# Channel-major projections: both parts of the activations streamed as 512 columns under one high weight tile

## The chip, the cores and the metric

The kernel runs on one core of one Trainium2 chip. The metric is the device time of one execution in microseconds (us); lower is better. Runs of the kernel before took 1342.85, 1344.12 and 1344.26 us, so the median is 1344.12 us.

## What is computed

Two layers of a decoder trunk, for 256 tokens of 1024 channels, all in float32. Cut to what matters here:

```python
def swiglu(x, w_gu, w_down):                     # w_gu: 1024 x 5632, w_down: 2816 x 1024
    gate, up = jnp.split(x @ w_gu, 2, axis=-1)
    return (jax.nn.silu(gate) * up) @ w_down

def hybrid_layer(x, mem_n, ...):
    h = layer_norm(ALPHA * x + 0.5 * swiglu(x, ffn1_w_gu, ffn1_w_down), ...)
    (dn_q, dn_k, dn_v, dn_b, dn_a, dn_z, sw_q, sw_k, sw_v, xa_q, gates) = jnp.split(h @ w_in, split_idx, axis=-1)
    o_dn = deltanet_branch(...)                  # causal convolution + silu of q, k, v, then a chunked recurrence
    o_sw = sliding_window_attention(...)
    o_xa = memory_cross_attention(xa_q, mem_n, w_mem_kv)
    merged = jnp.sum(gates * jnp.einsum('bsnc,ncd->bsnd', branches, w_branch), axis=2)
    h = layer_norm(ALPHA * h + merged @ w_out, ...)
    return layer_norm(ALPHA * h + 0.5 * swiglu(h, ffn2_w_gu, ffn2_w_down), ...)
```

Each layer has two feed-forwards (`swiglu`) with the three mixers between them, so the whole has four feed-forwards and two mixer stages.

## The kernel before

**Split operands.** TensorE works on the type float32r here. To keep float32 accuracy every operand is split into a high part (a cast to float32r) and a low part (the value less its high part), and a product is three matmuls: high x high, high x low, low x high. `split` (L115) does this with one cast on ScalarE (ACT, L116) and one subtraction on VectorE (DVE, L117).

**Weights.** All weights come from HBM as one stream of units of 128 x 1024 numbers (512 KB) through `unit` (L99): a DMA on SyncE's queue into a ring of three raw buffers, then a `split` into a ring of five high (`whi`) and five low (`wlo`) tiles. A cast into a `whi` buffer waits until TensorE (PE) has done the matmuls of the unit five places earlier. Every unit costs one ACT cast and one DVE subtraction of 128 x 1024.

**Two kinds of projection.** `projA` (L140) is token-major: the activations are the stationary operand, 512 weight columns stream. It does the down-projections, gates, branch projections and the output projection. `projB` (L125) is channel-major: a 128 x 128 weight tile is the stationary operand and the 256 tokens of the transposed activations stream. For each of 8 row tiles k and each 128-channel tile t it issues three matmuls of 256 columns: L135 (high weights, high activations), L136 (high weights, low activations), L137 (low weights, high activations). All three add into the same 256 columns of a PSUM bank; a bank holds two channel tiles.

**Where projB is used.** In a feed-forward (`Ffn.rest`, L312) the columns f = 2..21 are done by one `projB` each, with two channel tiles (gate and up) and two weight units: 16 (k, t) pairs. Then `glu` (L305) takes the silu of the gate on ACT (L307) and multiplies by the up half on DVE (L309), both read from PSUM, and a `split` of 128 x 256 makes the operand of the down-projection. In a mixer stage `projB` makes the memory keys, the delta-net's k, q and v (followed by `conv`, L416: one scaled copy on ACT and three multiply-adds on DVE for each 128-channel tile, L421 and L424, read from PSUM), the two queries and the window's keys: five calls of four channel tiles and one of one tile on the stream, one of four on the memory.

**PSUM.** Eight banks: `acc` has four tiles of one bank, `at` and `sm` two each. `full_rows` (L177) takes four `acc` and one `at` for a down-projection of 256 x 1024: `a` and `b` for the first 128 tokens, `c`, part of `d` and `at` for the second.

**What sets the order.** The tile framework schedules the instructions onto in-order queues, one for each engine; weight splits have a raised priority, so they run ahead of other work. An instruction at the head of a queue that waits holds everything behind it on that engine.

Of the kernel before, what the change touches and what calls it, by code (L numbers as in the profile page):

```python
# [17 lines left out]
P = 128  # L18
# [20 lines left out]
def tile_trunk(ctx, tc, x, xT, mem, wst, lnp, memln, cvw, rows, cst, out):  # L39
# [8 lines left out]
    psA = ctx.enter_context(tc.tile_pool(name="psA", bufs=4, space=bass.MemoryType.PSUM))  # L48
# [13 lines left out]
    def acc():  # L62
        return T(psA, [P, 512], "acc")
# [61 lines left out]
    def projB(xt, nt, kpu, behind=None):  # L125
        banks = [acc().rearrange("p (t s) -> p t s", t=2) for _ in range((nt + 1) // 2)]
        for uu in range(KD // kpu):
            hi, lo = unit(behind=behind)
            for kk in range(kpu):
                k = uu * kpu + kk  # L130
                for t in range(nt):
                    c = (kk * nt + t) * P
                    o = banks[t // 2][:, t % 2, :]
                    lastt = t % 2 == 1 or t == nt - 1
                    nc.tensor.matmul(o, hi[:, c:c + P], xt[0](k), start=(k == 0 and t % 2 == 0), stop=False, skip_group_check=True)  # L135
                    nc.tensor.matmul(o, hi[:, c:c + P], xt[1](k), start=False, stop=False, skip_group_check=True)  # L136
                    nc.tensor.matmul(o, lo[:, c:c + P], xt[0](k), start=False, stop=(k == KD - 1 and lastt), skip_group_check=True)  # L137
# [51 lines left out]
    def new_hT():  # L189
        hi = T(pu, [P, KD, S], "hThi", F32R)  # L190
        lo = T(pu, [P, KD, S], "hTlo", F32R)
        return hi, lo

    def acc_of(t):
        return (lambda k: t[0][:, k, :], lambda k: t[1][:, k, :])

    def to_T(put, tb, src, q):
        # half q of src (P, 1024), token-major, to its place in the transposed pair
# [4 lines left out]
        hi, lo = put(q)  # L203
# [720 lines left out]
```

## Time and profile before

| | |
|---|---|
| median of 3 runs | 1344.12 us (1342.85 to 1344.26) |
| the profiled execution, first to last instruction | 1340.6 us |
| mean granted TensorE clock | 0.994 |
| PE / PEld busy | 97% / 89% of the span |
| DVE / ACT / POOL busy | 63% / 49% / 4% |
| read from HBM | 235.64 MB, 178 GB/s over the span |

The profiled execution's span is 3.5 us below the median of the runs; what lies before the first and after the last instruction is not in it.

A profile line names the program line, the engine, the operation, what it writes and reads, the shapes and the count; then the total busy time and the mean of one in ns, then idle time before them and what ended it. PE is TensorE's matmul, PEld its weight loads. The busy time of a matmul includes its way through the array, which overlaps with the next one, so the pace of matmuls is read from the distance of their starts in the timeline, not from the busy time.

### The profile page before, as it was taken

Reading aid. Unit: us, or ns where it says so; the run is one execution under the profiler, and the core shown is the slowest. Engines: PE = TensorE matmul, PEld = TensorE weight load, DVE = VectorE, ACT = ScalarE, POOL = GpSimd, SP = SyncE. Lnnn points to the kernel's source line nnn. Section 1 sums busy time; section 2 is a strip of 40 time slices with the busy share of each in tenths; the row PEclk is TensorE's granted clock in tenths of the full one; section 3 lists DMA queues with packets and bytes.
Section 4 is the critical chain, followed back from the end, with each engine's and each line's share of the span. In section 5 each row is a group of like instructions: output and inputs, shape, how many; then the busy total and the mean of one; then the engine's idle time right before and its main releaser. Section 6 shows DMA issues by size and latency. Waiting matters only on the chain.

```text
span 1340.6 us, 22696 instructions
## 1 busy us (share of the span) xinstructions
PE 1304.8 (97%) x9112; PEld 1190.9 (89%) x9112; DVE 851.1 (63%) x1346; ACT 662.3 (49%) x1015; POOL 49.1 (4%) x75
## 2 busy tenths in 40 slices
PE   8999999999899999999999999999979999999997
PEld 7999889997678789998899998899977787999986
DVE  5585466777675775554665554757875758655545
ACT  6544344566464444444454443445656645444441
POOL 0000000102001000000000000000020010000000
PEclk9999999999899999999999999999999999999999
DMA  8867565653235736555665555566532457465553
GB/s 262 267 201 250 188 204 168 211 179 89 81 126 170 230 127 206 180 188 188 220 219 190 188 179 190 182 186 208 158 105 74 140 188 236 126 191 187 183 188 116
DMA packets 68585, 240.39 MB, mean 179 GB/s; under 512 B 8160, under 2 KB 9312, under 8 KB 68480
## 3 DMA queue, kind: packets, MB, share of 16 engines
q1 hardware_dynamic: 66176, 232.53, 54.0%
q0 software_dynamic: 2304, 6.43, 1.6%
q8 instruction: 71, 1.16, 0.4%
q14 instruction: 34, 0.28, 0.1%
HBM read 235.64 MB, written 3.28 MB: 178 GB/s over the span
## 4 chain that ended last, share of the span: by engine, by line
PE 77%; DMA 9%; DVE 8%; ACT 3%; issue 2%; POOL 1%; SPq 0%; DVEq 0%; ACTq 0%; POOLq 0%
PE acc L136 15%; PE acc L135 15%; PE acc L137 15%; PE acc L122 8%; PE acc L121 8%; PE acc L123 8%; DMA raw<-in_wst_dram 7%; DVE wlo L117 3%; ACT whi L116 2%; DMA w<-dr 1%; PE sm L644 1%; PE at L123 1%; PE at L121 1%; PE at L122 1%; PE sm L202 1%
## 5 line engine op out<-in xcount | busy, mean ns | idle before, releaser
L117 DVE TENSOR_TENSOR wlo<-raw,whi 128x1024 fp32r<-128x1024 f32 (+2 forms) x403 | 484.9, 1207 | 359.5 <-ACT whi L116 356.5
L116 ACT CAST whi<-raw 128x1024 fp32r<-128x1024 f32 (+2 forms) x403 | 414.9, 1033 | 413.0 <-DMA raw<-in_wst_dram 111.9
L135 PE MATMUL acc<-hThi,whi 128*128 128x256 f32 x1616 | 458.1, 284 | 0.0
L136 PE MATMUL acc<-hTlo,whi 128*128 128x256 f32 x1616 | 457.5, 283 | 0.0
L137 PE MATMUL acc<-hThi,wlo 128*128 128x256 f32 x1616 | 457.3, 283 | 0.0
L136 PEld LDWEIGHTS acc<-hTlo,whi 128*128 128x128 f32 x1616 | 310.3, 192 | 0.0
L135 PEld LDWEIGHTS acc<-hThi,whi 128*128 128x128 f32 x1616 | 310.3, 192 | 0.0
L137 PEld LDWEIGHTS acc<-hThi,wlo 128*128 128x128 f32 x1616 | 310.1, 192 | 0.0
L122 PE MATMUL acc<-wlo,u 128*128 128x512 f32 (+1 forms) x400 | 149.8, 375 | 0.0
L121 PE MATMUL acc<-whi,u 128*128 128x512 f32 (+1 forms) x400 | 149.0, 372 | 0.0
L123 PE MATMUL acc<-whi,u 128*128 128x512 f32 (+1 forms) x400 | 147.8, 371 | 0.0
L121 PE MATMUL acc<-whi,hThi 128*128 128x512 f32 (+1 forms) x272 | 103.5, 381 | 5.2 <-ACT whi L116 5.2
L122 PE MATMUL acc<-wlo,hThi 128*128 128x512 f32 (+1 forms) x272 | 103.2, 379 | 0.0
L123 PE MATMUL acc<-whi,hTlo 128*128 128x512 f32 (+1 forms) x272 | 103.1, 379 | 0.0
L121 PEld LDWEIGHTS acc<-whi,u 128*128 128x128 f32 x400 | 75.4, 188 | 13.8 <-DVE t L309 0.8
L122 PEld LDWEIGHTS acc<-wlo,u 128*128 128x128 f32 x400 | 75.4, 189 | 12.5
L123 PEld LDWEIGHTS acc<-whi,u 128*128 128x128 f32 x400 | 74.9, 188 | 12.7
L116 ACT CAST u<-t 128x256 fp32r<-128x256 f32 x80 | 32.5, 406 | 99.5 <-DVE t L309 99.3
L121 PEld LDWEIGHTS acc<-whi,hThi 128*128 128x128 f32 x272 | 52.2, 192 | 14.9 <-ACT whi L116 5.2
L123 PEld LDWEIGHTS acc<-whi,hTlo 128*128 128x128 f32 x272 | 51.9, 191 | 9.6 <-issue 1.6
L122 PEld LDWEIGHTS acc<-wlo,hThi 128*128 128x128 f32 x272 | 52.0, 191 | 8.6 <-DVE wlo L117 0.9
L117 DVE TENSOR_TENSOR u<-t,u 128x256 fp32r<-128x256 f32 x80 | 34.0, 425 | 32.6 <-ACT u L116 32.6
(312 smaller groups left out, 1489.0 us busy)
## 6 DMA issues: line engine op xcount, KB each, us to landing
raw<-in_wst_dram SPq DMA_DIRECT2D x409, 512.0 KB, 3.6
raw<-in_wst_dram SPq DMA_DIRECT2D x16, 324.0 KB, 3.1
gB<-in_lnp_dram SPq DMA_DIRECT2D x6, 512.0 KB, 6.3
bB<-in_lnp_dram SPq DMA_DIRECT2D x6, 512.0 KB, 5.7
mdr<-w POOLq DMA_DIRECT2D x4, 512.0 KB, 8.6
w<-dr POOLq DMA_DIRECT2D x4, 512.0 KB, 9.0
w<-mdr POOLq DMA_DIRECT2D x4, 512.0 KB, 5.6
t<-in_xT_dram SPq DMA_DIRECT2D x4, 256.0 KB, 5.2
```

Source lines behind the costliest of these rows:

```text
L116: nc.scalar.copy(hi, src)
L117: nc.vector.tensor_tensor(lo, src, hi.bitcast(F32), op=ALU.subtract)
L121: nc.tensor.matmul(o, lh, rh, start=first, stop=False, skip_group_check=skip)
L122: nc.tensor.matmul(o, lh, rl, start=False, stop=False, skip_group_check=skip)
L123: nc.tensor.matmul(o, ll, rh, start=False, stop=last, skip_group_check=skip)
L135: nc.tensor.matmul(o, hi[:, c:c + P], xt[0](k), start=(k == 0 and t % 2 == 0), stop=False, skip_group_check=True)
L136: nc.tensor.matmul(o, hi[:, c:c + P], xt[1](k), start=False, stop=False, skip_group_check=True)
L137: nc.tensor.matmul(o, lo[:, c:c + P], xt[0](k), start=False, stop=(k == KD - 1 and lastt), skip_group_check=True)
L202: nc.tensor.transpose(ps[:, j * P:(j + 1) * P], src[:, k * P:(k + 1) * P], ident)
L644: together(lambda h: nc.tensor.matmul(ps[:, h, :], *f(h), start=True, stop=True))
```

## The change

Five things change together.

1. `new_hT` makes one tile in which the high and the low activations of a row tile k lie side by side: 512 columns. The memory's transposed tiles are laid out the same way.
2. `projB` issues two matmuls instead of three for each (k, t): one of 512 columns under the high weight tile (its result: high x high in the first 256 columns, high x low in the last 256 of a full PSUM bank), and one of 256 columns under the low weight tile into the first half. It takes at most two channel tiles a call, so calls of four become two calls of two with half the units each; the weights are laid out in memory to suit (`_stream`).
3. A new `total` adds the halves when they are read: an ACT copy of the second half to SBUF and a DVE addition of the first. What follows (`glu`, `conv`, `split`) then reads SBUF.
4. `acc` has two tiles of two banks instead of four of one; `full_rows`, the feed-forward's first columns and the gates share such tiles.
5. `glu` writes in place of its operands in `Ffn.rest`.

```diff
-    psA = ctx.enter_context(tc.tile_pool(name="psA", bufs=4, space=bass.MemoryType.PSUM))
+    psA = ctx.enter_context(tc.tile_pool(name="psA", bufs=2, space=bass.MemoryType.PSUM))
...
     def acc():
-        return T(psA, [P, 512], "acc")
+        return T(psA, [P, 2, 512], "acc")
...
     def projB(xt, nt, kpu, behind=None):
-        banks = [acc().rearrange("p (t s) -> p t s", t=2) for _ in range((nt + 1) // 2)]
+        b = acc().rearrange("p t (a s) -> p t a s", a=2)
         for uu in range(KD // kpu):
             hi, lo = unit(behind=behind)
             for kk in range(kpu):
                 k = uu * kpu + kk
                 for t in range(nt):
                     c = (kk * nt + t) * P
-                    o = banks[t // 2][:, t % 2, :]
-                    lastt = t % 2 == 1 or t == nt - 1
-                    nc.tensor.matmul(o, hi[:, c:c + P], xt[0](k), start=(k == 0 and t % 2 == 0), stop=False, skip_group_check=True)
-                    nc.tensor.matmul(o, hi[:, c:c + P], xt[1](k), start=False, stop=False, skip_group_check=True)
-                    nc.tensor.matmul(o, lo[:, c:c + P], xt[0](k), start=False, stop=(k == KD - 1 and lastt), skip_group_check=True)
-        return banks
+                    nc.tensor.matmul(b[:, t], hi[:, c:c + P], xt[2](k), start=k == 0, stop=False, skip_group_check=True)
+                    nc.tensor.matmul(b[:, t, 0], lo[:, c:c + P], xt[0](k), start=False, stop=k == KD - 1, skip_group_check=True)
+        return b[:, 0:nt]
+
+    def total(b):
+        y = T(p2, [P, b.shape[1], S], "t2", bufs=4)
+        nc.scalar.copy(y, b[:, :, 1])
+        nc.vector.tensor_tensor(y, y, b[:, :, 0], op=ALU.add)
+        return y
+
+    def projB_split(xt, parts, behind=None):
+        for i in range(2):
+            split(*(t[:, 2 * i:2 * i + 2, :] for t in parts), total(projB(xt, 2, 4, behind)))
...
     def full_rows():
-        a, b, c, d = (acc() for _ in range(4))
-        return [[a, b], [c, d[:, 0:S], at()[:, 0:S]]]
+        a, b = acc(), acc()
+        return [[a[:, 0], a[:, 1]], [b[:, 0], b[:, 1, 0:S], at()[:, 0:S]]]
...
     def new_hT():
-        hi = T(pu, [P, KD, S], "hThi", F32R)
-        lo = T(pu, [P, KD, S], "hTlo", F32R)
-        return hi, lo
+        t = T(pu, [P, KD, 2, S], "hT", F32R)
+        return t[:, :, 0, :], t[:, :, 1, :], t
...
             for f in range(2, NFT):
-                (b,) = projB(xt, 2, 4, behind if f == 2 else None)
-                hf = self.glu(b[:, 0, :], b[:, 1, :])
+                gu = total(projB(xt, 2, 4, behind if f == 2 else None))
+                hf = self.glu(gu[:, 0], gu[:, 1], gu[:, 0], gu[:, 1])
...
         def conv(seg, dst):
-            for i, b in enumerate(projB(xt, 4, 2)):
+            for i in range(2):
+                b = total(projB(xt, 2, 4))
```

**The ACT queue in the feed-forward.** One column f, near the end of the first layer's second feed-forward; `acc` is what `projB` wrote, `t` the SBUF tile, `u` the down-projection's operand, `whi` a high weight tile. Before:

```order
L116 CAST whi_6424<-raw_6423 128x1024 [waits DMAHW7_49,PE_49,Activation_49]
L307 ACTIVATE t_987_6280<-acc_6219 128x256 [waits PE_49,Activation_49]
L116 CAST u_989_6284<-t_988_6282 128x256 [waits DVE_49]
L116 CAST whi_6454<-raw_6453 128x1024 [waits DMAHW0_49,PE_49]
L116 CAST whi_6495<-raw_6494 128x1024 [waits DMAHW1_49,PE_49,Activation_49]
L307 ACTIVATE t_997_6348<-acc_6287 128x256 [waits PE_49,Activation_49]
```

The same place after the change, where L117 is the cast of `split`, L142 the copy of `total` and L326 the silu:

```order
L117 CAST whi_5716<-raw_5715 128x1024 [waits DMAHW1_49,PE_49,Activation_49]
L142 COPY t_949_5600<-acc_5555 128x512 [waits PE_49]
L117 CAST whi_5737<-raw_5736 128x1024 [waits DMAHW2_49,PE_49,Activation_49]
L326 ACTIVATE t_949_5600<-t_949_5600 128x256 [waits DVE_49]
L117 CAST u_941_5552<-t_949_5600 128x256 [waits DVE_49]
L117 CAST whi_5758<-raw_5757 128x1024 [waits DMAHW3_49,PE_49,Activation_49]
```

The two weight casts of a column used to stand together; now the copy comes between them, the silu waits for DVE instead of PE, and the operand's cast still waits for DVE.

**The DVE queue at the same place.** `wlo` is a low weight tile; L309 is the product of `glu`. Before:

```order
L117 TENSOR_TENSOR wlo_6425<-raw_6423,whi_6424 128x1024 [waits DMAHW7_49,PE_49,Activation_49]
L309 TENSOR_TENSOR t_988_6282<-t_987_6280,acc_6219 128x256 [waits Activation_49]
L117 TENSOR_TENSOR u_989_6284<-t_988_6282,u_989_6284 128x256 [waits Activation_49]
L117 TENSOR_TENSOR wlo_6455<-raw_6453,whi_6454 128x1024 [waits DMAHW0_49,PE_49,Activation_49]
L117 TENSOR_TENSOR wlo_6496<-raw_6494,whi_6495 128x1024 [waits DMAHW1_49,PE_49,Activation_49]
```

After, where L143 is the addition of `total`, L328 the product and L118 the subtraction of `split`:

```order
L118 TENSOR_TENSOR wlo_5717<-raw_5715,whi_5716 128x1024 [waits DMAHW1_49,PE_49,Activation_49]
L143 TENSOR_TENSOR t_949_5600<-t_949_5600,acc_5555 128x512 [waits Activation_49]
L118 TENSOR_TENSOR wlo_5738<-raw_5736,whi_5737 128x1024 [waits DMAHW2_49,PE_49,Activation_49]
L328 TENSOR_TENSOR t_949_5600<-t_949_5600 128x256 [waits Activation_49]
L118 TENSOR_TENSOR u_941_5552<-t_949_5600,u_941_5552 128x256 [waits Activation_49]
```

The addition stands behind one weight subtraction and the product behind the other.

**PE where the down-projection begins.** This is the place behind the last `projB` of the same feed-forward; `u` is the down-projection's stationary operand. Before, `acc_6489` to `acc_6492` are the four banks of `full_rows`, and `acc_6492` is the one that the last `projB` (`acc_6422`) filled:

```order
L137 MATMUL acc_6422<-hThi_4923,wlo_6455 128x256
L121 MATMUL acc_6489<-whi_6495,u_824_5127 128x512 [waits Activation_49]
...
L121 MATMUL acc_6491<-whi_6495,u_824_5127 128x512 [waits DVE_49]
...
L122 MATMUL acc_6489<-wlo_6516,u_824_5127 128x512
L121 MATMUL acc_6492<-whi_6495,u_824_5127 128x256 [waits DVE_49]
```

After, `acc_5712` and `acc_5713` are the two tiles of two banks, and `acc_5713` is the one that the last `projB` (`acc_5660`) filled:

```order
L136 MATMUL acc_5660<-hT_4448,wlo_5685 128x256
L122 MATMUL acc_5712<-whi_5716,u_793_4650 128x512 [waits DVE_49]
...
L124 MATMUL at_5714<-whi_5716,u_793_4650 128x256
L122 MATMUL acc_5712<-whi_5737,u_793_4650 128x512
...
L122 MATMUL at_5714<-whi_5737,u_793_4650 128x256
L122 MATMUL acc_5713<-whi_5716,u_793_4650 128x512 [waits DVE_49]
```

Before, fourteen matmuls (eleven of 512 columns, three of 256) stand between the last `projB` and the first one that needs its bank. Now sixteen do (twelve of 512, four of 256).

More of the change, by code (lines that the diff above doesn't have):

```diff
@@ L202, in to_T @@
             nc.tensor.transpose(ps[:, j * P:(j + 1) * P], src[:, k * P:(k + 1) * P], ident)
[L203 removed]
         ts = slice(tb * P, (tb + 1) * P)
[L205 removed]
+        ps = ps.rearrange("p (j t) -> p j t", j=4)
+        parts = put(q)
+        n = 4 // len(parts)
+        for i, (hi, lo) in enumerate(parts):
+            split(hi[:, :, ts], lo[:, :, ts], ps[:, i * n:(i + 1) * n])
     def rsqrt(y, v, t):
@@ L285, in both @@
         def both(self, hT):
-            self.bank = {tb: acc() for tb in range(2)}
+            self.bank = acc()
             for k in range(KD):
@@ L397, in mixers @@
         xt = acc_of(hT)
-        outs = [[acc()[:, :MOD // 2] for _ in range(2)] for _ in range(2)]
+        outs = [[b[:, j, :MOD // 2] for j in range(2)] for b in (acc(), acc())]
         projA(xt, MOD, 1, KD, outs, 3)
@@ L769, in mixers @@
                 js = slice(j * 512, (j + 1) * 512)
-                outs = [[acc()] for _ in range(2)]
+                outs = two()
                 projA(xt, 512, 2, KD, outs)
@@ L773, in mixers @@
                     nc.scalar.activation(gt[tb][:, js], outs[tb][0], AF.Tanh, scale=0.5)
-            outs = [[acc() for _ in range(2)] for _ in range(2)]
+            outs = [[b[:, 0], b[:, 1]] for b in (acc(), acc())]
             def merge(tb, outs):
```

55 lines of the change are left out of this document (28 added, 27 removed).

## Prediction

> **What bounds the kernel now.** I read the page's first two parts, then the groups by shape, then the starts of matmuls in the timeline, then the other engines by window. The profiled execution spans 1340.6 us; the median of the runs, 1344.12, is 3.5 us more, which I carry over unchanged.
>
> ```profile
> span 1340.6 us, 22696 instructions
> PE 1304.8 (97%) x9112; PEld 1190.9 (89%) x9112; DVE 851.1 (63%) x1346; ACT 662.3 (49%) x1015; POOL 49.1 (4%) x75
> PE   8999999999899999999999999999979999999997
> PEclk9999999999899999999999999999999999999999
> ## 4 chain that ended last, share of the span: by engine, by line
> PE 77%; DMA 9%; DVE 8%; ACT 3%; issue 2%; POOL 1%; SPq 0%; DVEq 0%; ACTq 0%; POOLq 0%
> ```
>
> TensorE is busy at its granted clock in all slices but the beginning, the two delta-net places and the end, and 77% of the last chain is PE. So the pace of matmuls decides, and the first question is what one costs from start to start. Two stretches of the timeline hold matmuls of one width alone: the second feed-forward (256 columns, 86 rows from the first to the last shown) and the gates and branches (512 columns, 46 rows).
>
> ```profile
> 559.75 0.28 PE L135 MATMUL acc<-hThi,whi 128*128 128x256 f32 x1
> ...
> 569.95 0.28 PE L136 MATMUL acc<-hTlo,whi 128*128 128x256 f32 x1
> ```
>
> ```profile
> 411.73 0.39 PE L121 MATMUL acc<-whi,u 128*128 128x512 f32 x1
> ...
> 421.93 0.39 PE L121 MATMUL acc<-whi,hThi 128*128 128x512 f32 x1
> ```
>
> That is 10.20 us / 85 = 0.1200 us and 10.20 / 45 = 0.2267 us. Twice the columns cost 0.1067 more, so a matmul costs 0.0133 us whatever its width. This fixed part is what the change can save: the bytes, the multiplications and the weight units stay.
>
> How often? The groups by shape:
>
> ```profile
> L136 PE MATMUL acc<-hTlo,whi 128*128 128x256 f32 x1616 | 457.5, 283 | 0.0
> L136 PE MATMUL acc<-w,whi 128*128 128x256 f32 x64 | 18.4, 288 | 0.0
> L117 DVE TENSOR_TENSOR u<-t,u 128x256 fp32r<-128x256 f32 x80 | 34.0, 425 | 32.6 <-ACT u L116 32.6
> ```
>
> The 1616 + 64 = 1680 matmuls of L136 disappear into those of L135. The feed-forwards have 80 columns f (one operand split each) of 16 pairs (k, t), which is 1280; the mixers have the other 400.
>
> **The change part by part.** *Matmuls.* A pair (k, t) costs 3 x 0.1200 = 0.360 us now, and a column f 16 x 0.360 = 5.76 us. If a matmul costs the same among others of another width, the pair becomes 0.2267 + 0.1200 = 0.3467 us and the column 5.55 us. The saving is 0.0133 x 1680 = 22.4 us: 17.1 in the feed-forwards and 5.3 in the mixers.
>
> No row shows the two widths in turn. The nearest is the down-projection, where six matmuls of 256 columns follow nine of 512:
>
> ```profile
> 160.52 0.39 PE L123 MATMUL acc<-whi,u 128*128 128x512 f32 x1
> 160.75 0.28 PE L121 MATMUL acc<-whi,u 128*128 128x256 f32 x1
> 160.86 0.28 PE L122 MATMUL acc<-wlo,u 128*128 128x256 f32 x1
> ...
> 161.46 0.40 PE L121 MATMUL acc<-whi,u 128*128 128x512 f32 x1
> 161.69 0.40 PE L122 MATMUL acc<-wlo,u 128*128 128x512 f32 x1
> 161.93 0.39 PE L123 MATMUL acc<-whi,u 128*128 128x512 f32 x1
> ...
> 163.53 0.28 PE L121 MATMUL acc<-whi,u 128*128 128x256 f32 x1
> ```
>
> The first 256 behind a 512 takes 0.11 us, less than 0.12; the first 512 behind a 256 takes 0.23, the second 0.24. The whole round takes 2.78 us (160.75 to 163.53) where 6 x 0.1200 + 9 x 0.2267 = 2.76, so a change of width to and fro costs 0.02. For widths in turn the bounds are 0.2267 + 0.11 = 0.337 (the row of the first 256, with full-speed 512s) and 0.24 + 0.12 = 0.36 (the worst 512 with the slow 256). I take 0.347: the sum of the two constants, and nearly that of the two "first behind the other" rows (0.23 + 0.11 = 0.34). Savings at the bounds: 0.023 x 1680 = 39 us and 0.
>
> The Trainium skill, "TensorE: Matmul & The Clock Gate", section "Back-to-back issue gap", gives a fixed part of only about 2.5 ns for each matmul; by that the sum would be an estimated 0.0025 x 1680 = 4 us, and the change hardly worth it. Here the fixed part is 13.3 ns by the two stretches above, in a stream in which each matmul has a weight load of its own.
>
> *DVE and ACT.* What `total` adds has near twins in the groups:
>
> ```profile
> L117 DVE TENSOR_TENSOR wlo<-raw,whi 128x1024 fp32r<-128x1024 f32 x385 | 470.2, 1225 | 340.7 <-ACT whi L116 337.7 <-PE acc L137 1.4 <-PE acc L136 0.9
> L309 DVE TENSOR_TENSOR t<-t,acc 128x256 f32<-128x256 f32 x88 | 36.5, 415 | 3.4 <-ACT t L307 3.4
> L117 DVE TENSOR_TENSOR u<-acc,u 128x512 fp32r<-128x512 f32 x8 | 5.3, 685 | 1.2 <-ACT u L116 1.2
> L424 DVE SCALAR_TENSOR_TENSOR t<-acc,cw,t 128x254 f32<-128x254 f32 x24 | 11.0, 478 | 0.4
> L116 ACT CAST whi<-raw 128x1024 fp32r<-128x1024 f32 x385 | 401.9, 1048 | 394.6 <-DMA raw<-in_wst_dram 110.3 <-PE acc L136 101.0 <-PE at L123 82.9
> L307 ACT ACTIVATE t<-acc 128x256 f32<-128x256 f32 x88 | 33.2, 377 | 0.2 <-PE acc L137 0.2
> L116 ACT CAST u<-t 128x256 fp32r<-128x256 f32 x80 | 32.5, 406 | 99.5 <-DVE t L309 99.3
> L393 ACT COPY u<-acc 128x512 f32<-128x512 f32 x4 | 2.3, 584 | 1.2 <-PE acc L123 1.2
> ```
>
> The copy costs about 0.58 us of ACT (L393), the addition 0.69 of DVE (the 128 x 512 subtraction from PSUM). For a column f DVE then has 2 x 1.225 + 0.69 + 0.415 + 0.425 = 3.98 us of 5.55, ACT 2 x 1.048 + 0.58 + 0.377 + 0.406 = 3.46. As both queues are in order and wait for each other, the loop counts too: a weight cast, which waits for its buffer (1.05), its subtraction on DVE (1.225, and the silu beside it), the product behind that (0.415), the operand's cast (0.41), the second weight cast (1.05), the copy (0.58): 4.73 us. It fits in 5.55 with 0.8 left, so `total` costs nothing in the feed-forwards; the cover is that 0.8, and beyond it every microsecond is paid 80 times.
>
> *PSUM.* Counted from PE's end of a column, that loop begins at 2.78 (the buffer comes free after half of the next column); the copy of the next column then ends at 2.78 + 4.73 = 7.51, which is 2.0 after that column's own end at 5.55, and its addition, behind the second weight's subtraction, at 7.51 - 0.58 + 1.225 + 0.69 = 8.84, or 3.3 after. The column after the next needs the banks 5.55 after: 2.2 us to spare. At the end of a feed-forward the second tile is asked for after 12 x 0.2267 + 4 x 0.12 = 3.2 us: a wait of 0.1, four times. For that and the first column behind each norm I put 1 us in all.
>
> *Mixers.* There DVE is nearly full:
>
> ```profile
> 240.00:280.00 40.00, 40.00 (x335) 40.00 (x335) 29.81 (x42) 21.87 (x32) 2.11 (x1) 1.00 0.66 209
> 295.00:305.00 10.00, 10.00 (x70) 8.76 (x69) 9.73 (x33) 6.72 (x15) 2.04 (x2) 1.00 0.52 156
> 305.00:315.00 10.00, 9.27 (x63) 8.10 (x62) 8.90 (x26) 6.93 (x22) 0.00 (x0) 1.00 0.32 106
> 500.00:640.00 140.00, 140.00 (x1078) 135.74 (x1077) 77.03 (x92) 64.55 (x91) 0.00 (x0) 1.00 0.59 190
> ```
>
> The third busy column is DVE: 29.8 of 40 us in the projections, then 9.7 and 8.9 of 10 where the delta-net's chain begins, against 77 of 140 in a feed-forward. A half of `conv` has two weight subtractions, six multiply-adds of 0.478 and now an addition: 2.45 + 2.87 + 0.69 = 6.0 us of 5.55, so for four halves in a row DVE falls behind by about 2 us; the query halves (2.45 + 0.69 + 0.69 = 3.8) make it good. From 285 us on DVE sets the chain, and the additions of the last value half, the window keys and the last queries stand ahead of it: 0.69 + 0.42 + 2 x 0.69 = 2.5 us. Against that, calls of two tiles give their first half 5.5 us sooner, which takes one half of `conv` (2.9 us) out of the crowded place. Together about nothing; PE's 2.7 us a layer reach the chain only in part. Bounds for a layer: the whole 2.7 gained, or 2.5 lost. I count half the gain as lost: 2.6 of the 5.3.
>
> *Other edits.* The side-by-side tile, the in-place `glu` and the order of the units add no instruction to a feed-forward; the memory's transposes are split into twice as many smaller casts, once, under the first feed-forward's PE (`500:640` shows what room such a stretch has): nothing.
>
> The sum: 22.4 - 1 - 2.6 = 18.8 us, 1340.6 - 18.8 = 1321.8 for the span and 1325.3 with the 3.5 around it; I say 1325.
>
> **The rivals.** *The switch eats it* (chance 0.14). If each 512 behind a 256 costs 0.235 to 0.24, as in the rows above, and the 256 stays at 0.12, a pair costs 0.355 to 0.36 and saves 0.005 to 0: 8.4 to 0 us, less 3.6 for the edges and mixers: 1339 to 1348, in the middle 1343. For it: the 0.24 row. Against it: the 0.11 row. By the fixed part that the Trainium skill gives, the 4 us above, it would end there too, near no change.
>
> *Widths in turn are better than the sum* (0.10). Midway between the lower bound and my value a pair costs 0.342 and saves 0.018: 30 us less 3.6, 1317. For it: the 0.11 behind a 512, since now every 256 stands there. Against it: the 0.23 behind a 256, where now every 512 stands.
>
> *Slower: the change of width is paid in full* (0.07). Each pair changes width to and fro. If each pays the 0.02 us that the down-projection's round shows, it costs 0.367, and 0.007 x 1680 = 11 us are lost, with 3.6 more: 1359. It decides from 0.0133 on. Against it: in the round the loss lies on several 512s in a row, of which a pair has one.
>
> *Slower: the loop of ACT and DVE* (0.03). If its hand-overs add 1.5 us to the 4.73, a column takes 6.2 instead of 5.76 and 80 of them lose 35 us: 1379. It decides from 5.76 on. Now ACT idles in the loop for DVE 99.3 us in 75 times, the `u<-t` row, and that is in my sum.
>
> **How the numbers follow.** The forecast has 0.66, with 1318 to 1333 of its own (a mixer gain or loss of about 2.6 a layer, a pair between 0.344 and 0.350). Forecast and better case need 1312 to 1333; they hold 0.76, so the range goes up to 1340, which takes in the near end of the first rival. Below 0.2% (2.7 us) this kernel's measurement cannot tell a change from none. Faster: 0.66 + 0.10 + half of the first rival's 0.14 = 0.83; same: 0.05 of the other half; slower: the 0.02 that is left of it + 0.07 + 0.03 = 0.12.
>
> **What would show it.** Starts in a feed-forward that alternate 0.227 and 0.120, so 5.55 us a column; the window of a feed-forward full on PE, with DVE near 70%; the copy near 0.58 and the addition near 0.69; PE's waits around the delta-net within 3 us of now for a layer. Wrong would be: PE waiting for `acc` or `wlo` in a feed-forward (the loop), 512s at 0.235 and more (the switch), or waits at the delta-net longer by 5 us a layer.

## The result, and the profile after

The changed kernel takes 1355.63 us (median of 4 runs, 1351.30 to 1356.70), the kernel before beside it 1343.48 (4 runs, 1341.85 to 1344.26): the ratio is 1.0084, with a 95% interval of 1.0060 to 1.0108. The change makes the kernel slower by 12 us, 0.8%, with the interval clear of 1. (Of one experiment below, pool_pairs_evac, two of six runs, 1367.52 and 1370.06 us, were slow ones at a lower granted clock, 0.978 and 0.976 instead of 0.990 to 0.992, and its time is the median of the other four.) The profiled execution spans 1353.5 us against 1340.6. Its page:

```profile
span 1353.5 us, 19449 instructions
PE 1299.3 (96%) x7432; PEld 1105.5 (82%) x7432; DVE 909.6 (67%) x1456; ACT 715.7 (53%) x1125; POOL 48.6 (4%) x75
...
PE   8999999899799899999999999979997999999997
...
PEclk9999999899899999999999999999998999999999
```

PE has 1680 matmuls fewer and is busy 5.5 us less, yet the span grew by 12.9 us. The first sign is in the slices: PE and its clock have a new 8 in the eighth, from 237 us on, just behind the first layer's token-major values (a second new 8 of the clock is in the second layer's delta-net, from 1015 us). The next view is the page's groups (busy us, mean ns, then the idle time ahead of them and what ended it):

```profile
L135 PE MATMUL acc<-hT,whi 128*128 128x512 f32 x1616 | 573.0, 399 | 12.9 <-DVE swv L427 12.5
L136 PE MATMUL acc<-hT,wlo 128*128 128x256 f32 x1616 | 455.8, 282 | 0.0
...
L143 DVE TENSOR_TENSOR t<-t,acc 128x512 f32<-128x512 f32 (+1 forms) x106 | 71.4, 675 | 0.1
L142 ACT COPY t<-acc 128x512 f32<-128x512 f32 (+1 forms) x106 | 60.8, 573 | 5.5 <-PE acc L136 5.4
```

The copy and the addition cost what was put for them (0.57 and 0.68 us). But the projections now wait 12.5 us for `swv`, the DVE copy of the sliding window's values, which the change does not touch. In PE's waits (total, times, longest) before has no such row; it has the first row here as 12.9, 2, 6.9:

```profile
PE at L770 <- ACT pp L767: 14.8, 2, 7.5
PE acc L135 <- DVE swv L427: 12.5, 2, 6.9
```

Where the time went, by stage: from the first matmul of a stage to the first of the next, read from the starts in the timeline (us; the two numbers are the two layers).

| stage | before | after | change |
|---|---|---|---|
| first feed-forward, columns f = 2..21 | 117.8, 115.6 | 116.3, 113.7 | -1.6, -1.9 |
| its down-projection, norm, memory keys and values | 85.9, 86.1 | 87.1, 87.2 | +1.3, +1.1 |
| token-major b, a, z and window values | 14.5, 14.5 | 20.2, 21.5 | **+5.7, +7.0** |
| channel-major projections of the mixers | 60.5, 60.5 | 62.3, 63.2 | +1.8, +2.7 |
| rest of the mixers | 184.1, 182.8 | 186.4, 184.6 | +2.3, +1.8 |
| second feed-forward, columns f = 2..21 | 115.6, 115.6 | 111.7, 111.7 | -3.9, -3.9 |
| all else | | | +0.4 |

(Eight transposes, 0.9 us in each layer, stand behind the channel-major projections before and among them after; they move that much from "rest of the mixers" to the row above it.)

The columns of the feed-forwards gained 11.3 us. Everything between them lost 24 us, over half of it in one place. There, on PE (start, duration, and in brackets the wait that ended):

```profile
236.72 0.31 PE L124 MATMUL acc<-whi,hT 128*128 128x324 f32 x1
242.67 0.77 PE L135 MATMUL acc<-hT,whi 128*128 128x512 f32 x1 [5.64 <-DVE swv L427]
243.24 0.41 PE L136 MATMUL acc<-hT,wlo 128*128 128x256 f32 x1
243.45 0.63 PE L135 MATMUL acc<-hT,whi 128*128 128x512 f32 x1
...
246.65 0.42 PE L135 MATMUL acc<-hT,whi 128*128 128x512 f32 x1
...
247.03 0.40 PE L135 MATMUL acc<-hT,whi 128*128 128x512 f32 x1
```

PE stands still for 5.6 us and then runs its first pairs at 0.64 us each, almost half speed, because the granted clock has fallen: 0.50 in the window from 242.7 to 246.6 us (the number behind POOL's).

```profile
242.70:246.60 3.90, 3.90 (x12) 3.32 (x13) 0.03 (x1) 0.00 (x0) 2.00 (x2) 0.50 0.61 190
```

The seven pairs from 242.67 to 247.03 take 4.36 us instead of 7 x 0.347 = 2.43. In the second layer the wait is 6.9 us and ten pairs take 6.35 instead of 3.47. The half speed adds 1.9 + 2.9 = 4.8 us to the 12.5 of waiting. The Trainium skill, "TensorE: Matmul & The Clock Gate", section "What's actually happening", says that the array's clock drops to half after an idle window of about 3.4 us and comes back after about as long a busy one; this trace agrees, with 4.0 us at half speed (242.67 to 246.65) behind 5.6 us of idling, and 5.9 (913.00 to 918.89) behind 6.9 in the second layer.

Why is the copy late? First DVE before, around the same time:

```profile
235.59 0.17 DVE L406 COPY ba<-acc 128x8 f32<-128x8 f32 x1 [0.77 <-PE acc L123]
...
236.83 0.28 DVE L409 COPY swv<-acc 128x128 f32<-128x128 f32 x1
237.19 2.36 DVE L117 TENSOR_TENSOR wlo<-raw,whi 128x1024 fp32r<-128x1024 f32 x2
240.38 1.23 DVE L117 TENSOR_TENSOR wlo<-raw,whi 128x1024 fp32r<-128x1024 f32 x1 [0.83 <-ACT whi L116]
241.53 0.28 DVE L409 COPY swv<-acc 128x128 f32<-128x128 f32 x1
```

Then DVE and ACT after:

```profile
237.07 0.17 DVE L424 COPY ba<-acc 128x8 f32<-128x8 f32 x1 [1.41 <-PE acc L124]
...
237.35 2.36 DVE L118 TENSOR_TENSOR wlo<-raw,whi 128x1024 fp32r<-128x1024 f32 x2
241.10 1.22 DVE L118 TENSOR_TENSOR wlo<-raw,whi 128x1024 fp32r<-128x1024 f32 x1 [1.39 <-ACT whi L117]
242.25 0.48 DVE L427 COPY swv<-acc 128x128 f32<-128x128 f32 x2
```

```profile
236.22 2.18 ACT L117 CAST whi<-raw 128x1024 fp32r<-128x1024 f32 x2
240.03 1.04 ACT L117 CAST whi<-raw 128x1024 fp32r<-128x1024 f32 x1 [1.63 <-DMA raw<-in_wst_dram]
240.98 0.88 ACT L426 ACTIVATE u<-acc 128x196 f32<-128x196 f32 x3
```

Before, the copy of the first 128 tokens' window values (236.83) stands ahead of three weight subtractions, and that of the second 128 tokens behind them. After, both stand behind them. The third subtraction waits for its cast, and the cast for a load that has not landed. So a small read at the end of two in-order queues holds an accumulator that PE needs at once. Why the scheduler gives the read this place is not shown.

### The profile page after: what moved, and what is told of

It reads as the page before. It is cut to its first block, busy times and chain, and to the rows that moved or that the text cites. A ratio compares the mean times of both kernels' runs of the same rounds, so it can differ in the third digit from the quotient of the medians.

```text
span 1353.5 us, 19449 instructions
## 1 busy us (share of the span) xinstructions
PE 1299.3 (96%) x7432; PEld 1105.5 (82%) x7432; DVE 909.6 (67%) x1456; ACT 715.7 (53%) x1125; POOL 48.6 (4%) x75
## 4 chain that ended last, share of the span: by engine, by line
PE 74%; DMA 10%; DVE 9%; ACT 4%; issue 3%; POOL 1%; SPq 0%; DVEq 0%; ACTq 0%; POOLq 0%
PE acc L135 27%; PE acc L136 14%; PE acc L122 8%; PE acc L124 8%; DMA raw<-in_wst_dram 8%; PE acc L123 8%; DVE wlo L118 3%; ACT whi L117 2%; DMA w<-dr 2%; PE at L122 1%; PE at L124 1%; PE at L123 1%; PE sm L661 1%; PE acc L299 1%; PE sm L216 1%
## 5 line engine op out<-in xcount | busy, mean ns | idle before, releaser
L118 DVE TENSOR_TENSOR wlo<-raw,whi 128x1024 fp32r<-128x1024 f32 (+2 forms) x403 | 485.5, 1209 | 314.1 <-ACT whi L117 311.2
L117 ACT CAST whi<-raw 128x1024 fp32r<-128x1024 f32 (+2 forms) x403 | 415.7, 1035 | 376.3 <-DMA raw<-in_wst_dram 93.6
L135 PE MATMUL acc<-hT,whi 128*128 128x512 f32 x1616 | 573.0, 399 | 12.9 <-DVE swv L427 12.5
L136 PE MATMUL acc<-hT,wlo 128*128 128x256 f32 x1616 | 455.8, 282 | 0.0
L135 PEld LDWEIGHTS acc<-hT,whi 128*128 128x128 f32 x1616 | 305.4, 189 | 85.9 <-issue 13.0
L136 PEld LDWEIGHTS acc<-hT,wlo 128*128 128x128 f32 x1616 | 307.6, 190 | 0.2
L122 PE MATMUL acc<-whi,u 128*128 128x512 f32 (+1 forms) x400 | 149.4, 373 | 0.0
L122 PE MATMUL acc<-whi,hT 128*128 128x512 f32 (+1 forms) x272 | 104.1, 384 | 5.0 <-ACT whi L117 5.0
L123 PE MATMUL acc<-wlo,hT 128*128 128x512 f32 (+1 forms) x272 | 103.8, 382 | 0.0
L124 PE MATMUL acc<-whi,hT 128*128 128x512 f32 (+1 forms) x272 | 103.7, 381 | 0.0
L122 PEld LDWEIGHTS acc<-whi,u 128*128 128x128 f32 x400 | 75.3, 188 | 14.1 <-DVE t L143 0.8
L117 ACT CAST u<-t 128x256 fp32r<-128x256 f32 (+1 forms) x92 | 39.8, 433 | 83.2 <-DVE t L328 83.1
L143 DVE TENSOR_TENSOR t<-t,acc 128x512 f32<-128x512 f32 (+1 forms) x106 | 71.4, 675 | 0.1
L142 ACT COPY t<-acc 128x512 f32<-128x512 f32 (+1 forms) x106 | 60.8, 573 | 5.5 <-PE acc L136 5.4
L122 PEld LDWEIGHTS acc<-whi,hT 128*128 128x128 f32 x272 | 52.4, 193 | 13.0 <-ACT whi L117 5.0
L123 PEld LDWEIGHTS acc<-wlo,hT 128*128 128x128 f32 x272 | 52.3, 192 | 9.9 <-issue 1.6
L124 PEld LDWEIGHTS acc<-whi,hT 128*128 128x128 f32 x272 | 52.4, 193 | 9.4 <-issue 1.6
L118 DVE TENSOR_TENSOR u<-t,u 128x256 fp32r<-128x256 f32 (+1 forms) x88 | 39.2, 448 | 30.7 <-ACT u L117 30.7
```

The costliest lines, as they stand in the source:

```text
L117: nc.scalar.copy(hi, src)
L118: nc.vector.tensor_tensor(lo, src, hi.bitcast(F32), op=ALU.subtract)
L122: nc.tensor.matmul(o, lh, rh, start=first, stop=False, skip_group_check=skip)
L123: nc.tensor.matmul(o, lh, rl, start=False, stop=False, skip_group_check=skip)
L124: nc.tensor.matmul(o, ll, rh, start=False, stop=last, skip_group_check=skip)
L135: nc.tensor.matmul(b[:, t], hi[:, c:c + P], xt[2](k), start=k == 0, stop=False, skip_group_check=True)
```

## The experiments

The suspicion falls on the accumulators, the fourth item of the change: with two tiles of two banks, a tile is free only when both its banks have been read. Theory A says that these paired tiles, and the places that the reads get with them, make the waits; the rivals put them on the new matmuls or on the addition on reading. In the texts of expectation "pair" is one (k, t): a matmul of 512 columns and one of 256.

"Waits" below are the distances between starts of neighbouring matmuls less the price of the width, where over 60 ns, added up over a profile: 54.2 us before, 82.0 after. They hold the losses at half speed too. Their size depends by a few us on the price taken for the narrow matmuls; it is the differences, which move by about 1 us, that the text uses.

### pool_pairs: the paired tiles alone

```diff
-    psA = ctx.enter_context(tc.tile_pool(name="psA", bufs=4, ...
+    psA = ctx.enter_context(tc.tile_pool(name="psA", bufs=2, ...
-        return T(psA, [P, 512], "acc")
+        return T(psA, [P, 2, 512], "acc")
...
-        banks = [acc().rearrange("p (t s) -> p t s", t=2) for _ in range((nt + 1) // 2)]
+        pair = acc().rearrange("p b (t s) -> p b t s", t=2)
+        banks = [pair[:, i] for i in range((nt + 1) // 2)]
```

> The kernel before with one part of the change alone: accumulator tiles of two banks (two of them) instead of four of one bank. The projections keep their three matmuls of 256 columns, and nothing is added on reading. Theory A (the paired tiles, not the new matmuls, make TensorE wait where the token-major b, a, z and window values hand over to the delta-net's keys): the wait of 5.8 and 7.1 us that the changed kernel shows there comes here as well, with the matmuls behind it at half speed for some us, so 10 to 18 us slower than before, 1353 to 1361 us. Rival B (the wait belongs to the new projections or to the addition on reading): within 3 us of before, 1340 to 1347 us, and no wait above 1 us at that place.

Measured: 1365.31 us, ratio 1.0164 (1.0143 to 1.0186), 22 us slower than before with before's own matmuls, and 4 us beyond the upper end of A's range. PE's waits:

```profile
PE acc L136 <- DVE swv L418: 9.8, 2, 4.9
...
PE acc L136 <- DVE swk L117: 5.7, 2, 2.9
```

The wait for `swv` is here without a single new matmul or addition; B falls. The second row is one that A had not named: the last query projection waits for the split of the window's keys, which holds the other tile. In all the waits grew from 54.2 to 75.8 us, the whole of the 22.

On ACT the cause can be seen as a matter of places. Before, the two silus of the first 128 tokens (L408, the first row) and one of the second stand ahead of the three casts:

```profile
234.85 0.66 ACT L408 ACTIVATE u<-acc 128x316 f32<-128x316 f32 x2
...
236.12 1.99 ACT L116 CAST whi<-raw 128x1024 fp32r<-128x1024 f32 x2
239.30 1.05 ACT L116 CAST whi<-raw 128x1024 fp32r<-128x1024 f32 x1 [1.19 <-DMA raw<-in_wst_dram]
240.26 0.32 ACT L408 ACTIVATE u<-acc 128x196 f32<-128x196 f32 x1
```

With paired tiles only the first silu does, and the one that reads the tile's second bank stands behind the casts:

```profile
235.60 0.43 ACT L417 ACTIVATE u<-acc 128x316 f32<-128x316 f32 x1
236.17 1.99 ACT L116 CAST whi<-raw 128x1024 fp32r<-128x1024 f32 x2
239.22 1.04 ACT L116 CAST whi<-raw 128x1024 fp32r<-128x1024 f32 x1 [1.06 <-DMA raw<-in_wst_dram]
240.18 0.88 ACT L417 ACTIVATE u<-acc 128x196 f32<-128x196 f32 x3
```

### evac_first: the reads ahead of the weight splits

```diff
         for tb in range(2):
             a, b = outs[tb]
-            nc.vector.tensor_copy(ba[:, tb, :], a[:, 0:8])
+            with tc.high_priority(offset=600):
+                nc.vector.tensor_copy(ba[:, tb, :], a[:, 0:8])
...
+                nc.vector.tensor_copy(swv[:, tb, :], b[:, 196:324])
```

> The changed kernel with one edit: the reads of the token-major b, a, z and window values (two copies on DVE and two silus on ACT for each 128 tokens) are put ahead of the weight splits. Theory A: the wait of TensorE for these reads goes (12.9 us in both layers) and with it the half-speed matmuls behind it (about 4.5 us), so 1355.6 - 17 = 1338 to 1341 us, 2 to 5 us below before. Rival B (the next weight units are late there anyway, since their loads wait for a free raw buffer): the wait stays above 3 us in each layer and is put down to a weight cast, 1347 us or more.

Measured: 1339.50 us, ratio to before 0.9966 (0.9948 to 0.9983), 16 us below the changed kernel. In the first layer the projection follows at once:

```profile
236.79 0.31 PE L124 MATMUL acc<-whi,hT 128*128 128x324 f32 x1
236.94 0.40 PE L135 MATMUL acc<-hT,whi 128*128 128x512 f32 x1
```

In the second, 2.2 us are left of the wait, now put down to the copy of b and a (`ba`), and the granted clock stays at 1.00 behind it (895 to 900 us). A holds: moving eight small reads in each layer gives back more than the change had lost.

### evac_two_and_two, evac_unit_wide: fewer changes of width

The trace of the changed kernel has a second surprise: a pair does not always cost the same. In the second feed-forward:

```profile
558.13 0.39 PE L135 MATMUL acc<-hT,whi 128*128 128x512 f32 x1
558.36 0.28 PE L136 MATMUL acc<-hT,wlo 128*128 128x256 f32 x1
558.47 0.39 PE L135 MATMUL acc<-hT,whi 128*128 128x512 f32 x1
```

In the first feed-forward of the next layer:

```profile
740.06 0.40 PE L135 MATMUL acc<-hT,whi 128*128 128x512 f32 x1
740.30 0.28 PE L136 MATMUL acc<-hT,wlo 128*128 128x256 f32 x1
740.42 0.40 PE L135 MATMUL acc<-hT,whi 128*128 128x512 f32 x1
740.65 0.28 PE L136 MATMUL acc<-hT,wlo 128*128 128x256 f32 x1
740.77 0.40 PE L135 MATMUL acc<-hT,whi 128*128 128x512 f32 x1
741.00 0.28 PE L136 MATMUL acc<-hT,wlo 128*128 128x256 f32 x1
741.12 0.40 PE L135 MATMUL acc<-hT,whi 128*128 128x512 f32 x1
```

The first shows 0.230 + 0.117 = 0.3467 us a pair, on and on; the second a cycle of three pairs from 740.06 to 741.12, 1.06 / 3 = 0.3533. The two experiments change the order of the matmuls on top of evac_first: two of 512 and then two of 256 for each row tile, or eight and eight for each weight unit.

```diff
                 for t in range(nt):
                     c = (kk * nt + t) * P
                     nc.tensor.matmul(b[:, t], hi[:, c:c + P], xt[2](k), ...
+                for t in range(nt):
+                    c = (kk * nt + t) * P
                     nc.tensor.matmul(b[:, t, 0], lo[:, c:c + P], xt[0](k), ...
```

> As evac_first, and in the projections the two matmuls of 512 columns of a row tile stand together, then the two of 256: the width changes half as often, everything else is equal. In the changed kernel a pair (512 and 256) costs 346.7 ns in the second feed-forwards and 353.3 ns elsewhere. Theory C (each change of width can cost something, so fewer changes cost less): 346.7 ns or less per pair everywhere, 7 us below evac_first. Rival D (the two prices have nothing to do with the change of width): 353 ns stays in the first feed-forwards and the mixers, within 2 us of evac_first.

> As evac_first, and in the projections the eight matmuls of 512 columns of a weight unit stand together, then the eight of 256: the width changes an eighth as often. Theory C: the pair at 346.7 ns or less everywhere, 7 us or more below evac_first. Rival D: as evac_first within 2 us. The high weights of a unit are let go no earlier than before, the low ones are wanted 1.6 us later, so no wait should come from that.

Measured: 1330.04 us (0.9898, 0.9873 to 0.9923) and 1334.96 (0.9932, 0.9914 to 0.9950). A pair costs 348.3 ns in every undisturbed stretch of the first and 349.2 of the second: neither price of the changed kernel, and in between. So C and D both fail on the price. Nor do the times follow from it: two_and_two gained 9.5 us, of which the waits make 7.0 (66.5 to 59.5 us): 2.5 at the second layer's token-major values and 2.7 among the first layer's branch projections are the largest parts, and neither place has a matmul in the new order.

### single_tiles: the change with one-bank tiles

```diff
-    psA = ... bufs=2 ...
+    psA = ... bufs=4 ...
-        return T(psA, [P, 2, 512], "acc")
+        return T(psA, [P, 512], "acc")
...
-        nc.scalar.copy(y, b[:, :, 1])
-        nc.vector.tensor_tensor(y, y, b[:, :, 0], op=ALU.add)
+        for t, o in enumerate(b):
+            nc.scalar.copy(y[:, t], o[:, 1])
+            nc.vector.tensor_tensor(y[:, t], y[:, t], o[:, 0], op=ALU.add)
```

> The changed kernel with accumulators of four tiles of one bank again: a projection takes two of them, and the addition on reading takes two copies and two additions of 128 x 256 instead of one each of 128 x 512. The matmuls and their order in pairs are those of the changed kernel, and the reads of the window values get no raised priority. Theory A (the paired tiles made the waits): no wait above 1 us where the token-major values hand over to the delta-net's keys, TensorE's waits in all near before's 54 us, the matmuls 11 to 20 us cheaper than before by the two prices of a pair (353.3 and 346.7 ns): 1324 to 1336 us. Rival B (two halves of a bank are read later than one bank was, and this holds TensorE): waits stay near 80 us, 1345 us or more.

Measured: 1326.98 us, ratio 0.9882 (0.9854 to 0.9911): 16 us faster than before and 29 faster than the changed kernel, with the same matmuls and no raised priority. `swv` is early again, at 236.19:

```profile
236.19 0.28 DVE L425 COPY swv<-acc 128x128 f32<-128x128 f32 x1
236.67 2.36 DVE L118 TENSOR_TENSOR wlo<-raw,whi 128x1024 fp32r<-128x1024 f32 x2 [0.20 <-ACT whi L117]
```

The waits are 58.0 us. And the smaller reads are dearer than the ones they replace:

```profile
L143 ACT COPY t<-acc 128x256 f32<-128x256 f32 x210 | 76.6, 369 | 87.4 <-PE acc L136 87.2
...
L144 DVE TENSOR_TENSOR t<-t,acc 128x256 f32<-128x256 f32 x210 | 85.8, 416 | 15.9 <-ACT t L143 15.7
```

That is 76.6 + 85.8 = 162 us of ACT and DVE against 60.8 + 71.4 = 132 in the changed kernel, 30 us more work for 29 us less time: these engines are not what bounds it. A holds in full; this is the fastest of the versions measured here. But one-bank tiles are not the only way there: evac_two_and_two, with two paired tiles, takes 1330.04.

### pool_pairs_evac: is it the one place?

pool_pairs with the reads raised as in evac_first.

> pool_pairs (the kernel before with paired accumulators) with the reads of the token-major b, a, z and window values put ahead of the weight splits. Theory A in its narrow form (the paired tiles cost at this place alone): the waits of 5 us there go in both layers, with the half-speed matmuls behind them: 1343 to 1347 us. In its wide form (the paired tiles make waits at other borders too, such as 3.0 us ahead of the window's queries in each layer): 1347 to 1354 us.

Measured: 1350.44 us (median of four, 1347.20 to 1351.44), ratio 1.0047 (1.0029 to 1.0064). The wide form: of the 22 us that paired tiles cost the kernel before, 15 go with the one place, and 7 stay at other borders (the 3.0 us ahead of the window's queries, from start to start, are still there in both layers). In the changed kernel it is likewise: 16 of the 29 us go with evac_first, and most of the rest with the one-bank tiles or with the order of evac_two_and_two.

### total_twice: how much cover the addition has

```diff
             for f in range(2, NFT):
-                gu = total(projB(xt, 2, 4, ...))
+                b = projB(xt, 2, 4, ...)
+                total(b)
+                gu = total(b)
```

> evac_two_and_two with the copy and the addition on reading done twice in each feed-forward column, the first time into a tile that nobody reads: 0.58 us more of ACT and 0.69 of DVE a column. The step of the prediction that it tests: these two cost nothing, since the loop of weight cast, subtraction, product, operand cast, cast and copy takes 4.73 us of a column's 5.57. With the second copy it takes 5.31 and still fits: within 4 us of evac_two_and_two, 1326 to 1334 us, and TensorE full in the feed-forwards. Rival (the cover is thinner than that, as the hand-overs add to the loop): the columns get longer than 5.57 us, and each 0.1 us is paid 80 times: 1338 us or more.

Measured: 1353.11 us, ratio 1.0069 (1.0050 to 1.0089), 23 us above evac_two_and_two. The windows of the second feed-forward (PE is the third column, DVE the fifth by busy time), first evac_two_and_two, then total_twice:

```profile
500.00:590.00 90.00, 90.00 (x519) 78.54 (x518) 62.66 (x83) 52.26 (x82) 0.00 (x0) 1.00 0.62 198
```

```profile
500.00:590.00 90.00, 88.49 (x493) 75.09 (x492) 67.49 (x92) 59.62 (x94) 0.00 (x0) 1.00 0.61 192
```

A column in the steady part takes 5.89 us instead of 5.57 (the 15 columns from 523.81 to 612.11 take 88.30). So the expectation failed: of 0.58 + 0.69 = 1.27 us more, 0.31 come out at the end. What PE waits for at each new column is an accumulator: it goes on 0.15 us behind the end of the second addition, the last read of the tile that it needs.

```profile
528.56 0.68 DVE L145 TENSOR_TENSOR t<-t,acc 128x512 f32<-128x512 f32 x1
```

```profile
529.39 0.70 PE L135 MATMUL acc<-hT,whi 128*128 128x512 f32 x2
```

That addition stands behind a weight subtraction, 2.8 us behind the first one of its column (531.68 to 534.46), so an extra `total` delays the tile by more than its own 1.27 us. By the time added, the cover was 1.27 - 0.31 = 0.96 us, near the 0.8 of the prediction. But what broke is the release of the paired tiles and not the loop that the 0.8 came from, so that the two agree may be chance. One `total` a column is free, two are not, and neither DVE (75% busy) nor ACT (66%) is full when it breaks. With one-bank tiles the cover was not measured.

### single_tiles_2a2, ffn_only, single_ffn_only, single_ahead250: what the mixers' part is worth

single_tiles_2a2 is single_tiles with the order of evac_two_and_two. ffn_only and single_ffn_only are single_tiles_2a2 and single_tiles with the old `projB`, old weight layout and no `total` outside of the feed-forwards. single_ahead250 is single_tiles with one number changed:

```diff
-AHEAD = 300
+AHEAD = 250
```

> As single_tiles, with the matmuls of a row tile as two of 512 columns and then two of 256. From evac_two_and_two a pair costs 348.3 ns in this order in every stage, so the matmuls save 1680 x 11.7 = 19.7 us on before. Theory A: waits near before's 54 us, so 1322 to 1328 us, 2 to 8 us below evac_two_and_two, since the wait of 1.5 us in each layer behind the memory keys goes too. Rival (the smaller reads cost the mixers more than the tiles give): 1330 us or more.

> As single_tiles_2a2, but the change is made in the feed-forwards alone: the memory keys and the mixers' projections keep three matmuls of 256 columns and four channel tiles a call, with nothing added on reading. Theory E (the change's gain on TensorE in the mixers, 400 x 11.7 = 4.7 us, reaches the end): 4 to 6 us above single_tiles_2a2. Rival F (VectorE, which is nearly full there, sets the delta-net's chain, and the additions eat that gain): within 2 us of single_tiles_2a2, or below it. Against before it should save the feed-forwards' 1280 x 11.7 = 15 us: 1327 to 1331 us.

> single_tiles with the change in the feed-forwards alone: the memory keys and the mixers' projections keep three matmuls of 256 columns and four channel tiles a call, with nothing added on reading. In the other order of matmuls the same step was worth 1.3 us (1334.3 with the mixers changed, 1333.0 without). Rival F (the mixers' part is worth nothing at the end, since the additions stand on VectorE where it sets the chain): within 3 us of single_tiles, 1324 to 1330 us. Theory E (the mixers' part saves what it saves on TensorE, 4 to 5 us): 1331 to 1333 us.

> single_tiles with the priority of the weight splits raised by 250 places instead of 300: no work is added or left out, and on each engine 50 to 130 rows stand a place or a few elsewhere. A control: how far do TensorE's waits and the time move when nothing but the places of some instructions change? If the difference of 7.3 us between single_tiles and single_tiles_2a2 comes from such places, this kernel may lie up to 8 us off single_tiles, with another sum of waits than its 58 us, and pairs at the same three prices. If it comes from the order of the matmuls, this kernel stays within 2 us, 1325 to 1329 us.

| kernel | us | ratio to before | waits, us |
|---|---|---|---|
| single_tiles | 1326.98 | 0.9882 (0.9854 to 0.9911) | 58.0 |
| single_tiles_2a2 | 1334.28 | 0.9931 (0.9909 to 0.9954) | 65.6 |
| ffn_only | 1332.97 | 0.9925 (0.9896 to 0.9955) | 58.6 |
| single_ffn_only | 1333.28 | 0.9928 (0.9906 to 0.9950) | 55.9 |
| single_ahead250 | 1333.37 | 0.9933 (0.9908 to 0.9957) | 59.0 |

single_tiles_2a2 missed its expectation: the order that gained 9.5 us with paired tiles lost 7.3 with single ones. The control says how to take that: single_ahead250 has the same work, a few rows elsewhere in the queues, and lies 6.4 us off. Not all of this need be the places: its four runs spread from 1331.27 to 1336.13 us, its profiled execution is only 2.4 us longer than that of single_tiles (spans of 1329.1 and 1326.7), and the price of a pair is settled anew in each execution (next experiment). The mixers' part was worth -1.3 us in one order of matmuls and +6.3 in the other, so neither E nor F is shown; what it brings is no larger than what moves without any change of work. The feed-forwards' part alone brings 10 us in both, by ratios whose intervals leave out 1. That is less than the matmuls' 15 us (1280 x 11.7 ns) in the one and 12.8 in the other (half of its columns at each price), and the waits, 4.4 and 1.7 us longer than before's, make up most of the difference.

### single_again: the price of a pair

> single_tiles once more, unchanged, for its profile alone: which stages ran their pairs at 346.7 ns and which at 353.3? In the first profile the first layer's feed-forwards were at 353.3 and the second layer's at 346.7. If the price belongs to the program, the same stages show the same prices; if it is settled anew in each execution, one or more stages have changed sides, and the span moves by 2.1 us for each.

Mean ns from one 512 to the next in steady stretches:

| | first ff, layer 0 | mixers 0 | second ff 0 | first ff 1 | mixers 1 | second ff 1 |
|---|---|---|---|---|---|---|
| the changed kernel | 353 | 353 | 346.7 | 353 | 353 | 346.7 |
| evac_first | 353 | 346.7 | 346.7 | 346.7 | 353 | 353 |
| single_tiles | 353 | 346.7 | 353 | 346.7 | 353 | 346.7 |
| single_again | 353 | 346.7 | 353 | 346.7 | 346.7 | 353 |

(The table gives the price of a stage's longest stretch. In evac_first the first feed-forward changed to 346.7 for its last five columns, behind the transposes of the memory, and the mixers of layer 0 to 353 for their last 32 pairs; in both runs of single_tiles the first feed-forward of layer 0 had some two columns at 346.7 between two interruptions.) The same program changed sides in two stages, so the price is settled anew in each execution. In the trace of the changed kernel it only ever changes where PE has been interrupted, and stays to the next interruption. The single run took 1325.09 us.

## Why the prediction was wrong

It put the time at 1325 us, faster than before; it is 1355.6, slower. In the sum, 22.4 us were to be saved on matmuls and 3.6 lost elsewhere. Measured, 15.5 are saved and the waits grow by 82.0 - 54.2 = 27.8, which gives 12.3 of the 12.9 us by which the span grew. By its steps:

- **Matmuls, 22.4 us saved: right in kind, 15 in size.** The pair's price of 0.3467 us is met exactly in the second feed-forwards (640 pairs). The other 1040 pairs cost 0.3533: 640 x 13.3 + 1040 x 6.7 ns = 15.5 us. That lies inside the bounds of 0.337 and 0.36, and the value taken is one of two that exist. The 0.02 us for a change of width to and fro, read in the down-projection, was no price of the change at all in one of the two cycles and a third of it in the other.
- **DVE and ACT cost nothing in the feed-forwards: right.** PE is full there (59.96 of 60 us, next fence) and DVE at 68%; total_twice puts the cover at about 1.0 us where 0.8 was said. The step left the addition out of the loop; in total_twice the addition, as the read that frees the accumulator, is what PE waits for.

```profile
500.00:560.00 60.00, 59.96 (x343) 52.40 (x342) 40.92 (x54) 36.56 (x56) 0.00 (x0) 1.00 0.62 196
```

- **PSUM, "I put 1 us in all": this is the step that failed.** It followed the paired tiles through the feed-forward and its end, and there it was right: in the second feed-forward the addition ends 3.24 us behind its column (526.23 to 529.47), where 3.3 was said. It did not follow them to the border between the token-major values and the first key projection, where the same two tiles pass from one projection to the next. The change showed no edit of work at that place, only of the shape of `outs`, and the order of DVE and ACT there was not read. The runs put in place of that 1 us: 12.5 of waiting for `swv`, 4.8 of half speed behind it, and smaller waits at other borders, such as 2.5 where the memory's values wait for the additions of its keys (`PE acc L122 <- DVE t L143`; neither before nor single_tiles has this one). pool_pairs shows the wait for `swv` with the paired tiles alone, and evac_first shows it gone or short with the same tiles and the reads in other places.
- **Mixers, half of 5.3 us lost: neither shown nor refuted.** Behind the projections the stages lost 2.3 and 1.8 us, or 3.2 and 2.7 with the transposes that moved, where the bound was 2.5; but that kernel's mixers start behind half speed, and the experiments on the mixers scatter by more than the sum in question.
- **The rivals.** The slower side was given to a price of the width paid in full and to the loop of ACT and DVE; neither happened. The first rival, a pair at 0.355 to 0.36, came near for the 1040 pairs at 0.3533, but it reaches no further than no gain on the matmuls. The mechanism that decided had no rival of its own.

That the rest of the sum was nearly sound shows in single_tiles: without the paired tiles the change gives 1327.0, and 1325.1 in single_again. How near this comes to 1325 is partly luck: the matmuls save less there than forecast, and single_ahead250, with the same work, takes 1333.4.

## What to carry to other kernels

A change of a pool's shape is a change everywhere that the pool is used: list every border at which a tile passes from one user to the next, and read in the order of the queues what stands ahead of the last read that frees it. Fewer, larger tiles of the same bytes give the scheduler coarser things to wait for; here more and smaller reads (30 us more work on engines with room) went with a time 29 us shorter. The Trainium skill, "Perfetto Trace Analysis", section "Matmuls", asks that independent matmul groups rotate through different PSUM banks, so that one's reading overlaps the next. Here the same eight banks gave 1327.0 us with four tiles and 1355.6 with two, so the number of tiles that rotate matters beside the banks; evac_two_and_two comes to 1330.0 with two, so they are not the whole of it. And before a difference of some us between two schedules is explained, a control with the same work in other places shows what may come without any cause in the work: 6 us here.

## What the runs showed of the hardware beyond expectation

- One stream of instructions, alternating matmuls of 512 and 256 columns with a weight load each, has two steady paces, 346.7 and 353.3 ns a pair, taken up behind an interruption and kept until the next. What chooses between them stays open. Orders with fewer changes of width had one pace: 348.3 ns in twos, 349.2 in eights.
- At the lower clock behind an idle stretch five pairs take 3.20 us (243.45 to 246.65), 0.640 each and not twice 0.3467 = 0.693. By the prediction's constants the 768 columns alone make 3 x 0.1067 = 0.320 at the full clock, twice that is 0.640 at the granted clock of 0.50: the fixed 13.3 ns of a matmul do not show at the lower clock. The Trainium skill, "TensorE: Matmul & The Clock Gate", section "Wait — 56ns, not 53.3ns?", says the same of its own, smaller fixed part.
